# Choosing the keys of three long tiles in the retention stage instead of in sparse attention, with a reordered entry into the feed-forward part

## The chip, the cores and the metric

One core of a Trainium2 chip runs the whole program. The metric is the device time of one execution in microseconds (us), from which medians are taken over several runs. The engines are called TensorE (PE in the rows), VectorE (DVE), ScalarE (ACT), GpSimd (POOL) and SyncE (SP, which only issues transfers).

## The reference, cut to what matters

Two layers of a streaming encoder over one prompt of 1024 frames and 8 running streams of 16 frames. Both layers do the same:

- an input projection, split among three mixers that read the same rows;
- mixer A: a gated MLP that mixes positions within chunks of 128;
- mixer B: sparse attention. An indexer scores every admissible key for each query, the best 256 are kept (68 for the streams), and six heads attend over those keys;
- mixer C: retention, six heads in the chunkwise recurrent form, with a state that decays from chunk to chunk, a norm for each head and a gate;
- an output projection, `x = LN(ALPHA * x + mix @ w_out)`, then `x = LN(ALPHA * x + ffn(x))`, where the feed-forward part gates an up projection with a short causal convolution.

```python
score = jnp.where(adm[None], score, -jnp.inf)
_, idx = lax.top_k(score, k_sel)
logits = jnp.where(valid[:, :, None, None, :], logits, -jnp.inf)
p = jax.nn.softmax(logits, axis=-1).astype(v.dtype)

def step(r, kv_n):
    return chunk_decay[None, :, None, None] * r + kv_n, r
```

## The kernel before, in words

**Tiles.** The 1024 prompt rows are eight tiles of 128 rows and the 128 stream rows are a ninth. In the program's order tile number `DEC` = 4 is the streams', `G1` = 0 to 4 and `G2` = 5 to 8; in the score and attention code i = 0 to 7 counts prompt tiles and i = 8 the streams. Every product of float32 numbers is made of three matmuls with parts that split each operand exactly (`mm3`, L176 to L178); the high part is a cast on ScalarE, the low part a subtraction on VectorE or GpSimd (`put`, L1224; `load_slab`, L105).

**Order.** The text of the program sets a priority: an instruction that stands earlier in it is preferred. A planner runs over the whole program and writes one fixed order for each engine from these priorities and from its own estimate of when operands are ready. `high_priority(offset=-1500)` puts what it holds behind everything else that is ready; `issue_after(ins)` keeps what it holds behind one instruction of the same engine. On the chip every engine then works in the order written for it and waits where an operand is missing.

**One layer** has these stages: indexer and mixer A, retention, sparse attention in two parts, output projection and first norm, feed-forward entry, feed-forward loop over 22 column blocks, down projection and second norm.

**Selection.** Three searches, one for each group in `SETS` = ((2, 3, 4), (6, 7), (5, 8)), find each row's threshold bit by bit. They run during retention at the low priority (`searches`, `advance`, `chain`). After its search a tile is selected (`select`, L616): an equality test, a running count, two comparisons and one last step that turns 0 and 1 into a bias of the logits (L622 to L628), all on VectorE. A tile that isn't in `LATE` is selected in `chain`, still in retention, in place over its scores. A tile in `LATE` is selected in sparse attention, after the projection of a tile in `HEAVYJ` (`b_proj`, L891), into its own bias tile. Tiles 4 to 7 that are not in `LATE` are copied into their bias tiles at the end of the first part (L1129 to L1132), since the scores' memory is given up there.

**Retention** (`c_qk`, `c_turn`, `c_vg`, `c_out`, `c_norm`) goes over three head pairs p and nine tiles. `c_out` keeps the state: VectorE adds the new product to the decayed state `gR`, and GpSimd makes `gR` from the state (L777). `c_norm(2, 5)`, the last norm, is wholly on VectorE. The tiles of sparse attention's first part take the memory that retention gives up.

**Sparse attention, first part.** The projections of nine tiles are 19 steps (`steps`); `work()` makes the next one. `FIRST` of them come at once, the rest as filler in units of attention: after a unit in `EXTRA`, in the stream units in `DFILL`, and after chunk c of tile i where (i, c) stands in `FILLS`. A unit is `look` (logits, bias and minimum on VectorE L958, exponential on ScalarE L960, reciprocal, scale L962) and `gather` (turn the weights, copy them in two parts L991 and L992, multiply with the values L969 and L970). `look_dec` and `gather_dec` (L1059) are the like for streams. **Second part:** tiles 4 to 7, whose filler is the output projection of `G1`. The scale is on GpSimd for i of 4 and up.

**Output projection and norm.** `w_out` adds into the rows (L1163). `norm1(j)` of a tile in `G2` takes mean and variance (`row_stats`, L223 and L224), adds EPS on VectorE (L211), takes the power on GpSimd (L212), makes the bias on VectorE (L231) and applies both on ScalarE (L232).

**Feed-forward entry.** The product with the two weight halves is made of seven products (a Strassen-like form), whose operands are sums of row halves and sums of weight blocks. `half1(j)` makes the row operands of tiles in `G1`, `pair(j)` those of the others: eight turns on TensorE (L1236), four recovered blocks (L1276), eight affine steps on ScalarE (L1290), then sums on VectorE (L1292 to L1298), each split by `put`. The first sum `t1` lies in `tail` for all pairs. `pair` returns `rest`, which splits the last two sums. `wnext()` makes the next weight operand: for S2 three sums and for S4 one on GpSimd (L1358 to L1362), which also use `tail`, then a cast (L1364) and a subtraction (L1365); on its way it issues the next loads on SyncE (`raw_load`, L1341). Four `wnext` come after `w_out(8, 2)` and four after `w_out(8, 3)`; then come the products `early` (A11, A12 of block 0), a copy of the first to free its bank (L1449), `pair(8)`, two more products, and the rests.

```python
        early("A11", 0, "B11")
        nc.scalar.copy(s1, first["A11", 0][:, :, :288])
        early("A12", 0, "B21")
        rests.append(pair(8, where(), where()))
        early("A11", 1, "B11")
        early("A12", 1, "B21")
```

Of the kernel before, what the change touches and what calls it, by code (L numbers as in the profile page):

```python
# [37 lines left out]
LATE = (4, 5, 6, 7)  # L38
WOP = 7
FIRST = 5  # L40
EXTRA = (0, 2, 4)
DFILL = (0, 1, 2, 3)
FILLS = ((0, 0), (1, 0), (2, 0), (2, 1), (3, 3), (4, 1), (5, 1), (6, 1), (7, 1), (6, 5), (7, 5))
LOOKF = (4, 5, 6, 7)
HEAVYJ = (2, 3, 4, 7)
# [22 lines left out]
def hybrid_encoder(ctx: ExitStack, tc: tile.TileContext, d: dict):  # L68
# [145 lines left out]
    def row_stats(r, sp, st=None):  # L214


        halves = (0, 1) if st is None else (1,)
        if st is None:
            st = sp.tile([P, 2, 6], F32, tag="bnst", name="bnst", bufs=2)
        mv = sp.tile([P, 2], F32, tag="bnmv", name="bnmv", bufs=2)  # L220
        sc = sp.tile([P, 2], F32, tag="bnsc", name="bnsc", bufs=2)
        for c in halves:
            nc.vector.bn_stats(st[:, c, :], r[:, c * 512:(c + 1) * 512])  # L223
        nc.vector.bn_aggr(mv, st)  # L224
        rstd_of(sc[:, 0:1], mv[:, 1:2])
        return mv, sc

    def norm_rows(r, sp, st=None):

        mv, sc = row_stats(r, sp, st)  # L230
        nc.vector.scalar_tensor_tensor(sc[:, 1:2], mv[:, 0:1], -1.0, sc[:, 0:1], op0=ALU.mult, op1=ALU.mult)  # L231
        nc.scalar.activation(r, r, AF.Identity, bias=sc[:, 1:2], scale=sc[:, 0:1])  # L232
# [44 lines left out]
    for L in range(d["layers"]):  # L277
# [471 lines left out]
        def c_out(p, j, st):  # L749
# [3 lines left out]
            if j != DEC:  # L753
# [21 lines left out]
                if j < NT - 1:  # L775
                    st["gR"] = gR = cw.tile([P, P], F32, name="gR")
                    nc.gpsimd.tensor_scalar(gR, Rn, gch[:, 0, p:p + 1], None, op0=ALU.mult)  # L777
# [164 lines left out]
        def look(i, par, wp):  # L942
# [6 lines left out]
            for hh in range(3):  # L949
# [12 lines left out]
                (nc.vector if i < 4 else nc.gpsimd).tensor_scalar(pr[:, :w], pr[:, :w], st[:, 1:2], 1.0, op0=ALU.mult, op1=ALU.mult)  # L962
# [183 lines left out]
        lnT = ct[0][:, 1024:1040].rearrange("p (a k) -> p a k", a=2)  # L1146
        nc.sync.dma_start(lnT, d["ln1T"][L])
        bnj = {j: ct[0][:, 1040 + 12 * n:1052 + 12 * n].rearrange("p (c s) -> p c s", c=2) for n, j in enumerate(G2)}
# [75 lines left out]
        def put(at, n, src, eng):  # L1224

            nc.scalar.copy(at(n, 0), src)
            eng.tensor_tensor(at(n, 1), src, at(n, 0).bitcast(F32), ALU.subtract)
# [51 lines left out]

        def pair(j, where, rec):  # L1280
# [4 lines left out]
            t1, t2, t3 = (t.rearrange("p (k t) -> p k t", k=4) for t in (tail[:, 0:512], *temps))  # L1285
            temps[:] = x1s[j][:, 0:512], x1s[j][:, 512:1024]
            b11, b21 = whole(at, ("B11", "B21"), rec)
            for k0, t, v in ((0, t3, va), (4, t2, vb)):
                for k in range(4):
                    nc.scalar.activation(t[:, k, :], v[:, k, :], AF.Identity, bias=lnT[:, 1, k0 + k:k0 + k + 1],  # L1290
                                         scale=lnT[:, 0, k0 + k:k0 + k + 1])
# [4 lines left out]
            V.tensor_tensor(t2, t2, t1, ALU.subtract)  # L1296
            put(at, "T2", t2, V)
            V.tensor_tensor(t2, b21, t2, ALU.subtract)  # L1298

            def rest():  # L1300
                put(at, "T3", t3, V)
                put(at, "T4", t2, V)

            return rest
# [39 lines left out]
        def wnext():  # L1344
# [11 lines left out]
            src = {"A11": a11, "A12": a12, "S1": tail[:, 0:512], "S2": a11, "S3": a21, "S4": a12, "A22": a22}[n]  # L1356
            if n == "S2":
                G.tensor_tensor(tail[:, 0:512], a21, a22, ALU.add)  # L1358
                G.tensor_tensor(a21, a11, a21, ALU.subtract)
                G.tensor_tensor(a11, tail[:, 0:512], a11, ALU.subtract)  # L1360
            if n == "S4":
                G.tensor_tensor(a12, a12, a11, ALU.subtract)  # L1362
# [21 lines left out]
        for u, (s, j) in enumerate(todo_w):  # L1384
# [19 lines left out]
            if s == 3 and j > 5:  # L1404
                rests.append(pair(j - 1, where(), where()))
            if j == 8 and s >= 2:
# [44 lines left out]
        rests.append(pair(8, where(), where()))  # L1451
# [3 lines left out]
        for r in rests:  # L1455
            r()
# [363 lines left out]
```

## Time and profile before

| | |
|---|---|
| median of 3 runs | 2881.7 us (2879.95 to 2882.68) |
| the profiled execution | 2882.72 us, of which the span from first to last instruction is 2880.9 |
| mean granted clock of TensorE | 0.988 |
| TensorE busy | 2793.0 us, 97% of the span, 19444 matmuls |
| VectorE busy | 2061.6 us, 72% |
| ScalarE busy | 1387.3 us, 48% |
| GpSimd busy | 886.3 us, 31% |

The matmuls are pipelined, so a busy TensorE need not be at its peak. Idle time of another engine costs nothing by itself. In the rows a line is L and its number, a tile has the program's name without its buffer number, and `<-` stands between what is written and what is read; a wait is put down to what ended it. The two layers start at 0 and about 1430 us, and the second repeats the first's waits at much the same places.

### The profile page before, as it was taken

How to read it: one execution, taken by the hardware profiler on the slowest of the kernel's cores; microseconds unless marked ns; L12 is line 12 of the kernel's file. 1: busy time of each engine (PE TensorE's matmuls, PEld its weight loads, DVE VectorE, ACT ScalarE, POOL GpSimd, SP SyncE). 2: the span in 40 equal slices, each digit the busy share in tenths (PEclk: the TensorE clock that was granted, in tenths of full speed). 3: DMA queues.
4: the chain of work that ended last, by engine and by line, in shares of the span. 5: the costliest groups of instructions: out<-in, count | busy, mean ns of one | idle time of the engine just before them, and what ended most of it. 6: DMA issues, size and time to landing. Idle time of an engine off the chain costs nothing. (4 is left out here: it accounts for less than half of the span.)

```text
span 2880.9 us, 51251 instructions
## 1 busy us (share of the span) xinstructions
PE 2793.0 (97%) x19444; PEld 2613.9 (91%) x19444; DVE 2061.6 (72%) x4580; ACT 1387.3 (48%) x2937; POOL 886.3 (31%) x891
## 2 busy tenths in 40 slices
PE   8999999998999999999999999989989999999998
PEld 8898898998999999888898988989889999997886
DVE  6899878768666666556678997787686666665656
ACT  5687656645333333421256885565553333334211
POOL 2334543443322232000433445334432223220003
PEclk9999999999999999999999999999999999999999
DMA  4121123132212222443212111231322121224421
GB/s 138 53 66 50 43 62 102 58 125 92 72 70 76 76 79 96 158 131 127 79 47 81 39 50 47 56 111 47 121 94 77 69 85 70 72 100 155 153 84 66
DMA packets 105013, 243.15 MB, mean 84 GB/s; under 512 B 21671, under 2 KB 42047, under 8 KB 104767
## 3 DMA queue, kind: packets, MB, share of 16 engines
q1 hardware_dynamic: 88014, 198.59, 21.3%
q10 hardware_dynamic: 16752, 41.29, 3.7%
q8 instruction: 153, 2.51, 0.3%
q14 instruction: 94, 0.76, 0.1%
HBM read 185.20 MB, written 54.64 MB: 83 GB/s over the span
## 5 line engine op out<-in xcount | busy, mean ns | idle before, releaser
L176 PE MATMUL pg<-ar,ring 128*128 128x288 f32 x1408 | 417.1, 296 | 10.1 <-ACT s L1449 4.2
L178 PE MATMUL pg<-ar,ring 128*128 128x288 f32 x1408 | 417.2, 296 | 0.0
L177 PE MATMUL pg<-ar,ring 128*128 128x288 f32 x1408 | 416.5, 296 | 0.0
L1364 ACT CAST ring<-raw 128x512 fp32r<-128x512 f32 x264 | 163.3, 622 | 422.8 <-PE pg L177 401.6
L128 POOL TENSOR_TENSOR ring<-raw,ring 128x512 fp32r<-128x512 f32 (+1 forms) x140 | 191.7, 1396 | 317.9 <-ACT ring L127 270.1
L571 ACT ACTIVATE spare<-sc,cand 128x896 bf16<-128x896 f32 (+5 forms) x262 | 244.7, 934 | 67.3 <-DVE cand L598 21.2
L176 PEld LDWEIGHTS pg<-ar,ring 128*128 128x128 f32 x1408 | 266.1, 189 | 11.7 <-ACT s L1449 4.6
L1365 DVE TENSOR_TENSOR ring<-raw,ring 128x512 fp32r<-128x512 f32 x264 | 203.7, 776 | 90.9 <-ACT ring L1364 90.9
L177 PEld LDWEIGHTS pg<-ar,ring 128*128 128x128 f32 x1408 | 266.2, 189 | 0.0
L178 PEld LDWEIGHTS pg<-ar,ring 128*128 128x128 f32 x1408 | 266.0, 189 | 0.0
L1540 DVE TENSOR_TENSOR s<-s,pg 128x576 f32<-128x576 f32 x220 | 164.4, 749 | 50.8 <-PE pg L178 48.3
L1650 DVE TENSOR_TENSOR acc<-acc,pdn 128x512 f32<-128x512 f32 x180 | 121.3, 683 | 89.3 <-PE pdn L178 88.7
L1484 DVE TENSOR_TENSOR hx<-s,pg 128x512 f32<-128x512 f32 x88 | 60.5, 688 | 150.5 <-PE pg L178 150.5
L176 PE MATMUL pwo<-ring,ar 128*128 128x256 f32 x576 | 166.9, 290 | 0.0
L177 PE MATMUL pwo<-ring,ar 128*128 128x256 f32 x576 | 163.8, 284 | 0.0
L178 PE MATMUL pwo<-ring,ar 128*128 128x256 f32 x576 | 163.8, 284 | 0.0
L565 DVE TENSOR_SCALAR_CACHE_REDUCE spare<-sc,cand 128x384 bf16<-128x384 f32 (+4 forms) x208 | 158.5, 762 | 1.9
L176 PE MATMUL pdn<-ring,ar 128*128 128x512 f32 x360 | 140.1, 389 | 0.0
L177 PE MATMUL pdn<-ring,ar 128*128 128x512 f32 x360 | 140.1, 389 | 0.0
L178 PE MATMUL pdn<-ring,ar 128*128 128x512 f32 x360 | 140.1, 389 | 0.0
L1489 ACT ACTIVATE ct<-hx,cwt 128x512 f32<-128x512 f32 x88 | 71.8, 816 | 127.7 <-DVE hx L1484 127.7
L176 PE MATMUL pvg<-ring,ar 128*128 128x256 f32 x432 | 127.8, 296 | 1.4 <-DVE sg L740 1.4
(427 smaller groups left out, 9434.7 us busy)
## 6 DMA issues: line engine op xcount, KB each, us to landing
raw<-w_gu SPq DMA_DIRECT2D x90, 512.0 KB, 3.8
ad<-ct ACTq DMA_DIRECT2D x44, 576.0 KB, 2.8
raw<-w_d SPq DMA_DIRECT2D x44, 512.0 KB, 4.3
raw<-w_s SPq DMA_DIRECT2D x40, 512.0 KB, 3.9
raw<-w_o SPq DMA_DIRECT2D x32, 512.0 KB, 4.0
araw<-ad SPq DMA_DIRECT2D x48, 288.0 KB, 3.0
s<-ad SPq DMA_DIRECT2D x40, 288.0 KB, 3.6
x1d<-x ACTq DMA_DIRECT2D x18, 512.0 KB, 2.6
```

The lines of the kernel that those rows point to most:

```text
L128: eng.tensor_tensor(l[:, t], raw[:, r], h[:, t].bitcast(F32), ALU.subtract)
L176: nc.tensor.matmul(out, lh, rh, start=first, stop=False)
L177: nc.tensor.matmul(out, lh, rl, start=False, stop=False)
L178: nc.tensor.matmul(out, ll, rh, start=False, stop=last)
L565: nc.vector.tensor_scalar(junkv[:, :w], sc[i], cand[q][:, c:c + 1].bitcast(F32), float(kof(i) - w), op0=ALU.is_lt, op1=ALU.add, accum_out= ...
L571: nc.scalar.activation(junka[:, :w], sc[i], AF.Sign, bias=cand[q][:, c:c + 1].bitcast(F32), scale=-1.0, accum_out=dst)
L1364: nc.scalar.copy(h, src)
L1365: V.tensor_tensor(l, src, h.bitcast(F32), ALU.subtract)
L1484: V.tensor_tensor(hp.rearrange("p (c n) -> p c n", c=2), prompt(sv), prompt(b), ALU.add)
L1489: nc.scalar.activation(cf[:, 512 * h:512 * h + 512], hp, AF.Identity, **kw)
L1540: V.tensor_tensor(out, a, b[:, :, :288], ALU.add)
L1650: V.tensor_tensor(acc[j][:, cs], acc[j][:, cs], po, ALU.add)
```

## The change

Four kinds of edits. First, of the four long tiles only tile 7 stays in `LATE`, and it is selected after the first projection (`HEAVYJ` = (0,)); tiles 4, 5 and 6 are selected in retention and copied later. Second, the fillers of sparse attention's first part are placed elsewhere: one place less in `EXTRA` and `DFILL`, and (3, 1) in place of (2, 1) in `FILLS`. Third, for the last head pair the decayed state is made on ScalarE, and for the last look of tile 7 the scale is made on VectorE. Fourth, at the feed-forward entry: the norm of a `G2` tile has all three small steps on GpSimd; `t1` has two buffers in `ct[0]` by turns, and the small vectors that lay there go to `tail`; the sums of weight blocks are on VectorE for block 0; four of the eight early `wnext` come after `pair(8)`, their casts behind its affine steps and their three sums behind its sum before T2; the rests of all pairs come as casts behind the affine steps of pair 8 and subtractions behind its T2.

```diff
-LATE = (4, 5, 6, 7)
+LATE = (7,)
-EXTRA = (0, 2, 4)
-DFILL = (0, 1, 2, 3)
-FILLS = ((0, 0), (1, 0), (2, 0), (2, 1), (3, 3), (4, 1), (5, 1), (6, 1), (7, 1), (6, 5), (7, 5))
+EXTRA = (0, 2)
+DFILL = (0, 1, 2)
+FILLS = ((0, 0), (1, 0), (2, 0), (3, 1), (3, 3), (4, 1), (5, 1), (6, 1), (7, 1), (6, 5), (7, 5))
-HEAVYJ = (2, 3, 4, 7)
+HEAVYJ = (0,)
...
-        rstd_of(sc[:, 0:1], mv[:, 1:2])
+        if len(halves) == 1:
+            nc.gpsimd.tensor_scalar(sc[:, 0:1], mv[:, 1:2], EPS, None, op0=ALU.add)
+            nc.gpsimd.tensor_tensor(sc[:, 0:1], sc[:, 0:1], mhalf[:, 0:1], ALU.pow)
+        else:
+            rstd_of(sc[:, 0:1], mv[:, 1:2])
...
-        nc.vector.scalar_tensor_tensor(sc[:, 1:2], mv[:, 0:1], -1.0, sc[:, 0:1], op0=ALU.mult, op1=ALU.mult)
+        if st is None:
+            nc.vector.scalar_tensor_tensor(sc[:, 1:2], mv[:, 0:1], -1.0, sc[:, 0:1], op0=ALU.mult, op1=ALU.mult)
+        else:
+            nc.gpsimd.tensor_scalar(sc[:, 1:2], mv[:, 0:1], sc[:, 0:1], -1.0, op0=ALU.mult, op1=ALU.mult)
...
-                    nc.gpsimd.tensor_scalar(gR, Rn, gch[:, 0, p:p + 1], None, op0=ALU.mult)
+                    if p == 2:
+                        nc.scalar.activation(gR, Rn, AF.Copy, scale=gch[:, 0, p:p + 1])
+                    else:
+                        nc.gpsimd.tensor_scalar(gR, Rn, gch[:, 0, p:p + 1], None, op0=ALU.mult)
...
-                (nc.vector if i < 4 else nc.gpsimd).tensor_scalar(pr[:, :w], pr[:, :w], st[:, 1:2], 1.0, op0=ALU.mult, op1=ALU.mult)
+                (nc.vector if i < 4 or (i, par) == (7, 1) else nc.gpsimd).tensor_scalar(
+                    pr[:, :w], pr[:, :w], st[:, 1:2], 1.0, op0=ALU.mult, op1=ALU.mult)
...
-        lnT = ct[0][:, 1024:1040].rearrange("p (a k) -> p a k", a=2)
+        lnT = tail[:, 512:528].rearrange("p (a k) -> p a k", a=2)
...
+        t1s = ct[0][:, 0:512], ct[0][:, 512:1024]
...
-            t1, t2, t3 = (t.rearrange("p (k t) -> p k t", k=4) for t in (tail[:, 0:512], *temps))
+            t1, t2, t3 = (t.rearrange("p (k t) -> p k t", k=4) for t in (t1s[j % 2], *temps))
...
-            V.tensor_tensor(t2, t2, t1, ALU.subtract)
-            put(at, "T2", t2, V)
+            hold["sum"] = V.tensor_tensor(t2, t2, t1, ALU.subtract)
+            hold["split"] = put(at, "T2", t2, V)
             V.tensor_tensor(t2, b21, t2, ALU.subtract)
 
-            def rest():
-                put(at, "T3", t3, V)
-                put(at, "T4", t2, V)
-
-            return rest
+            rests.extend(((at, "T3", t3), (at, "T4", t2)))
...
+            e = G if f else V
             if n == "S2":
-                G.tensor_tensor(tail[:, 0:512], a21, a22, ALU.add)
-                G.tensor_tensor(a21, a11, a21, ALU.subtract)
-                G.tensor_tensor(a11, tail[:, 0:512], a11, ALU.subtract)
+                with ExitStack() if f else tc.issue_after(hold["sum"].ins):
+                    e.tensor_tensor(tail[:, 0:512], a21, a22, ALU.add)
+                    e.tensor_tensor(a21, a11, a21, ALU.subtract)
+                    e.tensor_tensor(a11, tail[:, 0:512], a11, ALU.subtract)
             if n == "S4":
-                G.tensor_tensor(a12, a12, a11, ALU.subtract)
+                e.tensor_tensor(a12, a12, a11, ALU.subtract)
...
-            if j == 8 and s >= 2:
+            if (s, j) == (2, 8):
                 for _ in range(4):
                     wnext()
...
-        rests.append(pair(8, where(), where()))
+        pair(8, where(), where())
+        for _ in range(4):
+            with tc.issue_after(hold["affine"].ins):
+                wnext()
         early("A11", 1, "B11")
         early("A12", 1, "B21")
         rest_dec()
-        for r in rests:
-            r()
+        for at, n, t in rests:
+            with tc.issue_after(hold["affine"].ins):
+                nc.scalar.copy(at(n, 0), t)
+            with tc.issue_after(hold["split"].ins):
+                V.tensor_tensor(at(n, 1), t, at(n, 0).bitcast(F32), ALU.subtract)
```

## Rows read from the trace of the kernel before

**Rows 1.** Busy time by stretch: length, PE, PEld, DVE, ACT, POOL, PEclk, DMA

```profile
347.00:376.00 29.00, 29.00 (x232) 26.01 (x231) 14.87 (x38) 6.87 (x21) 17.63 (x16) 1.00 0.19 59
376.00:480.00 104.00, 93.38 (x747) 87.78 (x746) 85.56 (x235) 71.27 (x226) 34.69 (x38) 0.97 0.25 75
400.00:425.00 25.00, 21.61 (x179) 21.32 (x178) 24.78 (x64) 14.53 (x51) 7.01 (x7) 0.89 0.13 38
570.00:600.00 30.00, 26.75 (x198) 25.73 (x197) 26.54 (x60) 17.93 (x32) 18.37 (x14) 0.94 0.18 74
636.00:676.00 40.00, 31.07 (x223) 29.01 (x222) 33.11 (x59) 28.91 (x59) 13.02 (x14) 0.95 0.23 81
700.00:1180.00 480.00, 480.00 (x3559) 476.74 (x3558) 319.33 (x525) 188.16 (x299) 131.40 (x141) 1.00 0.25 85
...
1806.00:1912.00 106.00, 94.29 (x735) 88.74 (x734) 85.96 (x233) 70.70 (x221) 34.84 (x38) 0.94 0.24 74
...
2070.00:2116.00 46.00, 37.23 (x262) 35.42 (x260) 37.25 (x63) 33.94 (x69) 13.84 (x15) 0.93 0.24 86
```

**Rows 2.** TensorE's waits, 376 to 480 us: us in total, times, longest

```profile
PE tpd L1059 <- DVE ast L958: 3.4, 1, 3.4
...
PE pb L176 <- DVE ast L958: 1.4, 1, 1.4
```

**Rows 3.** The eight half-clock stretches, TensorE alone: one, and the sum

```profile
671.93:678.75 6.82, 5.41 (x22) 0.50 0.48 157
...
sum 40.95, PE 33.84; mean PE 4.23
```

**Rows 4.** VectorE on the bias tiles, 376 to 470 us; two steps by form

```profile
376.00:470.00 94.00, 24.72 (x20) 0.96 0.23 67
...
L627 DVE SCALAR_TENSOR_TENSOR bias<-sc,cand,bias 128x896 bf16<-128x896 f32 x1 | 3.3, 3301 | 0.0
...
L627 DVE SCALAR_TENSOR_TENSOR bias<-sc,cand,bias 128x1024 bf16<-128x1024 f32 x1 | 1.3, 1266 | 0.0
```

**Rows 5.** Timeline of ScalarE and TensorE where sparse attention begins

```profile
375.80 0.27 ACT L901 COPY kv<-pb 128x128 f32<-128x128 f32 x1 [4.55 <-DVE yb L819]
...
378.88 0.22 PE L173 MATMUL kt<-identr,kss 128*128 128x128 f32 x1
```

**Rows 6.** TensorE's waits, 570 to 600 us

```profile
PE po L969 <- ACT pth L991: 1.6, 1, 1.6
PE tp L988 <- POOL pr L962: 1.4, 1, 1.4
```

**Rows 7.** TensorE's waits at the first layer's feed-forward entry, 636 to 676 us

```profile
PE pg L176 <- ACT s L1449: 4.2, 1, 4.2
PE trx L1236 <- ACT x L232: 3.1, 2, 1.7
PE trx L1276 <- DVE x L1298: 1.4, 1, 1.4
```

**Rows 8.** TensorE's waits at the second layer's, 2070 to 2116 us

```profile
PE pg L176 <- DVE x L1298: 4.1, 1, 4.1
...
PE pg L176 <- ACT x L1290: 1.6, 1, 1.6
```

**Rows 9.** Timeline of ScalarE, VectorE and GpSimd at the first layer's entry

```profile
640.45 2.56 ACT L1290 ACTIVATE temp<-trx,ct 128x128 f32<-128x128 f32 x7 [0.75 <-PE trx L1236]
...
664.73 0.68 DVE L1227 TENSOR_TENSOR ar<-x,ar 128x512 fp32r<-128x512 f32 x1
...
665.50 1.60 DVE L1227 TENSOR_TENSOR art<-x,art 128x512 fp32r<-128x512 f32 x1
...
664.95 1.60 POOL L1358 TENSOR_TENSOR tail<-raw 128x512 f32<-128x512 f32 x1 [3.08 <-ACT ar L1226]
...
671.61 1.14 ACT L1364 CAST ring<-raw 128x512 fp32r<-128x512 f32 x2 [1.05 <-POOL raw L1362]
672.65 0.63 ACT L1449 COPY s<-pg 128x576 f32<-128x576 f32 x1
```

More of the change, by code (lines that the diff above doesn't have):

```diff
@@ L1145, in hybrid_encoder @@
         s1 = xp1.tile([P, 2, 288], F32, name="s1")
-        lnT = ct[0][:, 1024:1040].rearrange("p (a k) -> p a k", a=2)
+        lnT = tail[:, 512:528].rearrange("p (a k) -> p a k", a=2)
         nc.sync.dma_start(lnT, d["ln1T"][L])
-        bnj = {j: ct[0][:, 1040 + 12 * n:1052 + 12 * n].rearrange("p (c s) -> p c s", c=2) for n, j in enumerate(G2)}
+        bnj = {j: tail[:, 528 + 12 * n:540 + 12 * n].rearrange("p (c s) -> p c s", c=2) for n, j in enumerate(G2)}
         xg1s = ExitStack()
@@ L1226, in put @@
             nc.scalar.copy(at(n, 0), src)
-            eng.tensor_tensor(at(n, 1), src, at(n, 0).bitcast(F32), ALU.subtract)
+            return eng.tensor_tensor(at(n, 1), src, at(n, 0).bitcast(F32), ALU.subtract)
         def turned_x(src, where):
@@ L1289, in pair @@
                 for k in range(4):
-                    nc.scalar.activation(t[:, k, :], v[:, k, :], AF.Identity, bias=lnT[:, 1, k0 + k:k0 + k + 1],
+                    hold["affine"] = nc.scalar.activation(t[:, k, :], v[:, k, :], AF.Identity, bias=lnT[:, 1, k0 + k:k0 + k + 1],
                                          scale=lnT[:, 0, k0 + k:k0 + k + 1])
@@ L1404, in hybrid_encoder @@
             if s == 3 and j > 5:
-                rests.append(pair(j - 1, where(), where()))
-            if j == 8 and s >= 2:
+                pair(j - 1, where(), where())
+            if (s, j) == (2, 8):
                 for _ in range(4):
```

## The prediction

> **What bounds the kernel now.** I read the busy times by stretch first, then TensorE's waits in the stretches that show gaps, then the granted clock, and last the instructions at a few of those waits. In the feed-forward loop TensorE is never idle: 3559 matmuls fill 480 us, 0.135 us each [rows 1]. So nothing there can be won, and the change does not touch its steady part. The gaps lie in a few places of each layer: 10.6 us of 104 in sparse attention's first part, 3.25 of 30 near its end, 8.9 of 40 where the feed-forward part begins; the second layer has 11.7 of 106 and 8.8 of 46 in the like places [rows 1], and its own copy of the 3.25. Together that is 46.5 us. In the middle of the first of them VectorE works 24.78 of 25 us while TensorE stands for 3.4 [rows 1], and the two longest waits there end with VectorE [rows 2]. So VectorE, which is far from full over the whole run, is the bound in just these places.
>
> A second price hangs on them. The granted clock is 0.50 (1.2 of 2.4 GHz) in eight stretches of 3.4 or 6.8 us in or just behind these gaps, and TensorE is busy for 33.84 us of them [rows 3]. There 22 matmuls take 5.41 us, 0.246 each, against 0.135: 45% of busy time is lost, 15.2 us in all, 1.9 a stretch. The ceiling of the change is thus about 62 us.
>
> **Selection moved (LATE, HEAVYJ).** Choosing the keys of tiles 4 to 7 in sparse attention costs VectorE 24.7 us a layer, 20 steps of 1.2 on average [rows 4]. By width (640, 768 and 896 of 3328 columns) 69% of it, 17 us, goes into retention. Three copies into the bias tiles come in its place, on VectorE under projections; if that cover is gone they cost at most the average step each, 3.7 us. Tile 7's selection, the other 7.7 us, moves forward to the first projection, where four projections' matmuls are queued on TensorE; I neither credit nor charge it. Of the waits I credit those that end with the softmax minimum behind selection, 3.4 and 1.4 us, in both layers: 9.6. What is left of the idle time, 5.8 and 6.9 us, comes from the chain through three engines in tile 3's units, where no projection was left as filler.
>
> **Projections spread out (EXTRA, DFILL, FILLS).** Nothing is added: the 19 steps stay. By counting them, steps that came earlier now stand in the gathers of tile 3. Earlier units lose filler just as they lose VectorE's selection work. I credit a third of the rest, 1.9 and 2.3: 4.2 (ends 0 and 12.7). Of the clock, the two stretches behind the 3.4 us waits go wholly, two more in the second layer by a third: 1.3 + 3.8 = 5.1. This part: 18.9 us.
>
> **Price in retention.** Its last 29 us have 14.87 us of VectorE work, 14.1 free [rows 1], for 17 us of selection, at a lower priority than the rest. The overflow is 3 us. Sparse attention begins only when VectorE's last norm frees memory: ScalarE stood 4.55 us for it, and TensorE first needed the result 3.1 us after that wait ended [rows 5]. An instruction once begun is not interrupted, so the norm's steps queue behind selection steps of 1 to 2 us. Taken: 2.5 a layer, 5 in all (ends: none, and the third rival's price). The decayed state of the last head pair goes from GpSimd to ScalarE, which is busy 6.87 of 29 us there [rows 1]; no matmul waits for it in the rows: nothing, up to 1 us if ScalarE's queue is full.
>
> **Last softmax scale on VectorE.** TensorE waits 1.4 us for GpSimd's product there and then 1.6 for ScalarE's copy [rows 6]. VectorE is at 26.54 of 30 us, so the three products may only shift the wait. I take half of the 1.4, 0.7 a layer: 1.4 (ends 0 and, with the copy and its clock stretch, 4.9 a layer).
>
> **Entry of the feed-forward part.** The norm's chain now goes VectorE, GpSimd, VectorE, ScalarE; afterwards it stays on GpSimd before ScalarE. Two waits for it make 3.1 us a layer [rows 7]; one hop fewer of three, and no place in VectorE's queue: half of it, 1.55 a layer, 3.1 (ends 0 and 6.2). On GpSimd's queue the three steps stand among the stream pair's sums; it is busy 13.02 of 40 us there [rows 1], so I charge nothing. The load of the norm's vectors keeps its place on SyncE's queue and only changes its target.
>
> The other waits there are 4.2 + 1.4 in the first layer, 4.1 + 1.6 in the second [rows 7, 8]: 11.3. The trace shows what made them. A subtraction takes VectorE 0.68 us alone and 1.60 beside GpSimd's sum of 1.60; ScalarE's casts wait for GpSimd's sums, and the copy that frees TensorE's bank comes behind them, ending at 673.28 [rows 9]. The change takes all three causes away: sums of tile 0 on VectorE, four weight steps and all second halves behind pair 8's affine steps, two buffers for the first sums. SyncE's loads for the next tile move back with the weight steps; their first user is five products, 16 us, later, so that is covered.
>
> But something else is late next. From pair 8's transposes TensorE has two products, 48 matmuls, 6.5 us, until it needs the weight sum S2. The way to it: eight affine steps (2.56 us for seven, so 2.9 [rows 9]), four VectorE steps and three sums of 0.68, a cast of about 0.6 and a last 0.68: 8.9 us. A new wait of 2.4 stands in each layer. Net 11.3 - 4.8 = 6.5. Of the two clock stretches, 3.8, I credit half, 1.9. This part: 3.1 + 6.5 + 1.9 = 11.5 (ends: 21.3 if no wait follows, none if S2's wait takes everything back).
>
> Behind the waiting casts on ScalarE and sums on VectorE stand the second halves of the pairs, which the third to fifth product read: 7 us and more later.
>
> **The sum.** 18.9 + 1.4 + 11.5 - 5.0 = 26.8 us off the profiled execution's 2882.7 (span 2880.9): 2855.9. That execution lies 1.0 over the median of the runs shown, 2881.7, so 2855.
>
> **Rivals.** *Every gap closes* (0.20): the waits leave no follower and the clock stays up. Then of the 62 us some three quarters go, 46, and retention takes nothing back: 2836. For it: the waits share one cause. Against: the last third of sparse attention's gaps is a chain of engines, not load.
>
> *Selection was not the bound* (0.22): with filler taken from early units TensorE waits there for the same softmax, and of sparse attention only a third is won, 6; with 1.4 and 11.5, less 5, 14 us: 2868. For it: the units that lose filler are those with the 3.4 us wait.
>
> *Retention becomes VectorE's bound* (0.06), slower than before. The selection steps run at contended length: one on 896 columns takes 3.30 us, its like on 1024 only 1.27 [rows 4]. GpSimd works 17.63 of 29 us there, against 34.69 of 104 in sparse attention [rows 1]. At 2.2 times, 17 us become 37; less 14.1 free and 3.1 of slack, 20 us stall a layer, and a clock stretch makes 22. Both layers: 44, against 32 won: slower by 12, 2894. It decides from a stall of 16 a layer on. Against: TensorE is busy for all of retention's last 29 us [rows 1], although tiles 2, 3 and 8 are chosen in retention already. The Trainium skill, "SBUF — State Buffer", section "Who interferes with whom", makes this a rule: a VectorE instruction with two SBUF inputs, or one in a two-port mode, and a GpSimd instruction that reads SBUF shut each other out for a whole instruction. By that rule, moving selection to where GpSimd works more is wrong; the subtraction of 1.60 us beside GpSimd's 1.60 [rows 9] agrees with it. Taken whole it would give the rival's 2894 and not 2855; no run here shows what it costs TensorE.
>
> *The order hardly changes* (0.07): the planner puts the moved steps where they stood, and gains and price cancel: 2881.
>
> **How the numbers follow.** The forecast has 0.45. A measurement here tells about 0.2%, 5.8 us, from no change. Faster are the forecast, every gap closes and the selection rival: 0.87; the same 0.07; slower 0.06. Likeliest: 2855. The range holds the first three with a share of the unknown costs, from 2833 to 2877.
>
> **What would show it.** Right: no wait over 1 us for the softmax minimum in sparse attention's first units; no selection step behind its first projections except tile 7's; TensorE idle there under 5 us a layer; clock stretches down from eight to about four; at the entry a wait of some 2 us for S2 instead of 4.2 and 4.1; retention's last 29 us with VectorE near full. Wrong: sparse attention starting more than 5 us later after retention, new waits of the retention products for VectorE, or new half-clock stretches behind the S2 wait.

## The result and the profile after

The changed kernel takes 2901.43 us (median of 4 runs, 2899.35 to 2903.46), the kernel before 2882.19 on the same chip: a ratio of 1.0064, 95% interval 1.0052 to 1.0076. It is slower by 19.2 us, where 26.8 less were forecast. The profiled execution has a span of 2901.6 us against 2880.9. TensorE is busy for 2794.9 us of it, against 2793.0: of the 20.7 us more, 18.8 are idle time of TensorE. So new waits, not new work, made the loss.

The busy time by stretch of the changed kernel (columns as in [rows 1]; the first three stretches are the same, the last two longer, since the entry is):

```profile
347.00:376.00 29.00, 23.35 (x174) 20.18 (x173) 28.34 (x54) 7.12 (x23) 14.40 (x10) 0.93 0.03 10
376.00:480.00 104.00, 99.37 (x817) 96.55 (x817) 75.14 (x225) 71.84 (x227) 33.11 (x42) 0.97 0.28 80
570.00:600.00 30.00, 25.57 (x186) 24.64 (x185) 27.11 (x57) 16.34 (x29) 14.69 (x10) 0.89 0.17 71
636.00:700.00 64.00, 46.95 (x321) 45.04 (x320) 41.18 (x69) 37.34 (x75) 15.70 (x23) 0.89 0.18 62
2070.00:2140.00 70.00, 49.32 (x334) 47.41 (x333) 40.27 (x68) 36.90 (x74) 16.99 (x25) 0.88 0.17 57
```

Sparse attention's first part came out as meant: 4.6 us idle of 104 instead of 10.6, VectorE down from 85.56 to 75.14. The stretch before it lost what it had: TensorE, never idle in retention's last 29 us before, stands for 5.65 there, and VectorE is full. At the entry TensorE is idle for 17 of 64 us and 21 of 70.

TensorE's waits of the changed kernel, 340 to 480 us, the largest group (us in total, times, longest):

```profile
PE py L766 <- DVE Rb L777: 4.9, 2, 4.6
```

and 570 to 710 us:

```profile
PE pg L176 <- ACT ring L1375: 9.4, 1, 9.4
PE tp L999 <- DVE bnsc L211: 4.2, 1, 4.2
PE trx L1247 <- ACT x L239: 3.3, 1, 3.3
PE pg L176 <- DVE s L1557: 2.3, 1, 2.3
```

No wait for the softmax minimum is left ([rows 2] had 3.4 and 1.4). In their place stand one for the retention state (py), one for the last weights of tile 7 (tp, where [rows 6] had 1.4 and 1.6), one for the norm (trx, 3.3 for the 3.1 of [rows 7]) and the longest of all, 9.4 us before the first product with S2. The second layer repeats the four of them with 4.65, 4.23, 3.26 and 9.39 us, and has a fifth, before the first product of the entry and behind the last sum of a pair (L1311, L1298 before), where [rows 8] had 4.1:

```profile
PE pg L176 <- DVE x L1311: 5.3, 1, 5.3
```

The half-clock stretches, TensorE alone (granted clock 0.50 in each): thirteen in these places where [rows 3] had eight. Two of them, behind the waits for the state and for S2:

```profile
371.89:378.72 6.83, 5.29 (x25) 0.50 0.07 14
682.50:692.74 10.24, 5.88 (x24) 0.50 0.38 116
```

Stage by stage, from the start of each stage's first matmul in the two traces (layer one, layer two; us more than before; in the second layer the border between the third row and the fourth moves by up to 0.5 us with the matmul taken for it):

| stage | measured | forecast, both layers |
|---|---|---|
| retention, up to the first turn of keys | +9.2, +6.8 | +5.0 |
| sparse attention's first part from there | -9.9, -11.8 | -18.9 |
| second part (last scale on VectorE) | +1.1, +2.0 | -1.4 |
| norm, up to the recovered blocks of pair 5 | +2.6, +2.2 | -3.1 |
| the rest: entry, loop, down projection | +8.0, +13.9 | -8.4 |
| second layer's indexer stage | -3.3 | 0 |

### The profile page after: what moved, and what is told of

It reads as the page before. It is cut to its first block, busy times and chain, and to the rows that moved or that the text cites. A ratio compares the mean times of both kernels' runs of the same rounds, so it can differ in the third digit from the quotient of the medians.

```text
span 2901.6 us, 51222 instructions
## 1 busy us (share of the span) xinstructions
PE 2794.9 (96%) x19444; PEld 2622.1 (90%) x19444; DVE 2062.8 (71%) x4584; ACT 1391.4 (48%) x2951; POOL 860.3 (30%) x879
## 5 line engine op out<-in xcount | busy, mean ns | idle before, releaser
L128 POOL TENSOR_TENSOR ring<-raw,ring 128x512 fp32r<-128x512 f32 (+1 forms) x140 | 185.5, 1351 | 355.1 <-ACT ring L127 305.3
```

The source lines that it names most:

```text
L128: eng.tensor_tensor(l[:, t], raw[:, r], h[:, t].bitcast(F32), ALU.subtract)
```

## The experiments

Sixteen kernels ran, each beside runs of the kernel before on the same chip, so the ratio with its interval is what compares them (it differs from the quotient of the two medians by up to 0.07%).

| run | us | before | ratio, 95% interval |
|---|---|---|---|
| a_rests_free | 2894.8 | 2882.7 | 1.0048 [1.0033, 1.0063] |
| b_attention | 2880.1 | 2882.7 | 0.9995 [0.9986, 1.0005] |
| b_entry | 2895.2 | 2882.7 | 1.0048 [1.0033, 1.0063] |
| b_norm_scale | 2889.2 | 2882.7 | 1.0024 [1.0013, 1.0036] |
| fill_only | 2896.8 | 2882.1 | 1.0049 [1.0036, 1.0061] |
| late_67 | 2879.5 | 2882.1 | 0.9987 [0.9978, 0.9996] |
| gr_pool | 2877.9 | 2882.1 | 0.9981 [0.9972, 0.9990] |
| bufs_sums | 2888.1 | 2882.1 | 1.0018 [1.0009, 1.0027] |
| two_bufs | 2893.1 | 2882.6 | 1.0043 [1.0029, 1.0057] |
| entry_rests_free | 2889.4 | 2882.6 | 1.0025 [1.0015, 1.0034] |
| late_47 | 2877.2 | 2882.6 | 0.9984 [0.9975, 0.9992] |
| late_47_w | 2879.3 | 2882.6 | 0.9991 [0.9982, 1.0000] |
| one_buf_ct | 2890.1 | 2885.5 | 1.0020 [1.0011, 1.0030] |
| bufs_tail8 | 2884.6 | 2885.5 | 1.0001 [0.9992, 1.0010] |
| sums_only | 2882.2 | 2885.5 | 0.9990 [0.9980, 1.0000] |
| late_47_sums | 2878.9 | 2885.5 | 0.9982 [0.9973, 0.9990] |

### The change taken apart

**b_attention, b_entry, b_norm_scale**: the kernel before with one group of the edits each: selection, fillers and decayed state; the entry; the norm's small steps and the last scale.

> The kernel before with only the selection of tiles 4 to 6 in retention, the fillers' places and the decayed state on ScalarE. If the stages of the changed kernel add up: retention's end up to the turn of the keys +9.2 and +6.7 us, the rest of sparse attention's first part -9.9 and -11.8, so 2876 us, between 2872 and 2881, against 2882.2, with one wait of 4.7 us of the retention products for VectorE's state in each layer. Rival (the stages don't add up, the loss in retention needs the other edits too): no such wait, and 2860 to 2866.

> The kernel before with only the edits of the feed-forward entry: two buffers for the first sums, sums of S2 on VectorE, four weight steps and the second halves behind pair 8. Theory: it holds the main loss, a wait of some 9 us before the first S2 product in each layer, 2900 us, between 2895 and 2905. Rival (the wait needs the norm on GpSimd as well, which makes everything in the entry later): a wait of under 6 us and 2885 to 2892.

> The kernel before with only the norm's small steps on GpSimd and the last scale of tile 7 on VectorE. From the stages of the changed kernel: the scale +1 to +2 us a layer with one wait of about 4 us at the last transposes of the weights, the norm +2 to +3 a layer with one wait of about 3 us instead of two of 1.4 and 1.7: 2889 us, between 2885 and 2893. Rival (the norm's place on GpSimd helps when the rest of the entry is as before): 2881 or less.

Measured: -2.6, +12.5 and +6.5 us, together +16.4 of the 19.2. The first shows the waits expected (4.65 us for the state in each layer) and lies in the range expected; from no change it can't be told. The entry holds the main loss, with the wait of 9.38 us alone and no help from the norm. The third fell as expected, and its trace divides it: +1.2 and +1.8 us for the scale's stage, +2.6 and +2.2 for the norm's. Its rival (the norm helps when the rest is as before) is out.

### The wait for S2

What stands in the queues ahead of it, from the timeline of the changed kernel (start us, length, engine, line, operation, tiles, count, idle before):

```profile
672.98 1.18 ACT L1471 CAST ar<-temp 128x512 fp32r<-128x512 f32 x2
674.01 2.22 ACT L1471 CAST ar<-x 128x512 fp32r<-128x512 f32 x4
676.10 0.66 ACT L1237 CAST arb<-ct 128x512 fp32r<-128x512 f32 x1
679.44 0.69 DVE L1370 TENSOR_TENSOR raw<-raw 128x512 f32<-128x512 f32 x1
680.65 1.29 DVE L1473 TENSOR_TENSOR ar<-temp,ar 128x512 fp32r<-128x512 f32 x2
681.86 3.09 DVE L1473 TENSOR_TENSOR ar<-x,ar 128x512 fp32r<-128x512 f32 x5
685.47 0.68 DVE L1371 TENSOR_TENSOR raw<-tail,raw 128x512 f32<-128x512 f32 x1
686.86 0.61 PE L176 MATMUL pg<-art,ring 128*128 128x288 f32 x1 [9.38 <-ACT ring L1375]
```

The second halves of the pairs (L1471, L1473), which other products need only later, go first on both engines: six casts, 3.4 us, ahead of pair 8's own, and seven subtractions, 4.4 us, between the second sum of S2 (679.44) and the third (685.47). `issue_after` holds them behind pair 8's affine steps and its T2, but nothing holds them behind S2, and the planner placed them as soon as they were let go.

**a_rests_free**:

```diff
         for at, n, t in rests:
-            with tc.issue_after(hold["affine"].ins):
-                nc.scalar.copy(at(n, 0), t)
-            with tc.issue_after(hold["split"].ins):
-                V.tensor_tensor(at(n, 1), t, at(n, 0).bitcast(F32), ALU.subtract)
+            put(at, n, t, V)
```

> The changed kernel, but the second halves of all pairs (T3, T4) are made as before: nothing holds them behind pair 8. Theory (the place of these halves makes the wait): TensorE's wait before the first S2 product falls from 9.4 us to 2 to 3 in each layer, the wait of 2.3 to 2.8 us for the next weight subtraction goes, and with them about 2 us of half clock a layer: 2885 us, between 2880 and 2890, against 2901.4. Rival (the sums of S2 on VectorE make it, VectorE is full there whatever the order): the wait stays at 7 us or more and the time at 2897 or more.

TensorE's waits for the same two things in this run, 636 to 725 us:

```profile
PE pg L176 <- DVE s L1554: 3.1, 2, 2.1
PE pg L176 <- ACT ring L1375: 2.7, 1, 2.7
```

The wait falls from 9.4 to 2.7 us (2.25 in the second layer): the theory of the place holds, VectorE was not full whatever the order. But the loss against the kernel before fell by 7.1 us only, from 19.2 to 12.1, and not by 16, so the time lies above the range expected. A wait for VectorE comes at a later product instead of the 2.3 and 2.8 us of the changed kernel, 2.1 us in the first layer and 5.1 in the second, and the rest of the entry's loss lay elsewhere.

### The parts of the entry

**two_bufs** is the kernel before with the first of these edits (and the small vectors moved as in the change); **bufs_sums** has both; **entry_rests_free** is the whole entry with the second halves free as in a_rests_free.

```diff
-            t1, t2, t3 = (t.rearrange("p (k t) -> p k t", k=4) for t in (tail[:, 0:512], *temps))
+            t1, t2, t3 = (t.rearrange("p (k t) -> p k t", k=4) for t in (t1s[j % 2], *temps))
...
+            e = G if f else V
-                G.tensor_tensor(tail[:, 0:512], a21, a22, ALU.add)
+                e.tensor_tensor(tail[:, 0:512], a21, a22, ALU.add)
...
```

> The kernel before with two of the entry's edits: two buffers for the first sums (and the small vectors moved for it), and the sums of block 0 on VectorE. The eight weight steps and the second halves of the pairs stay where they were. If GpSimd's sums and the one buffer made the waits of 4.2 and 4.1 us, these fall under 2 us, no wait before the first S2 product comes up, and the time is 2870 to 2876. Rival (the waits only move on to ScalarE's casts and affine steps): the waits in the entry add up to what they were, within 2 us a layer, and the time is 2879 to 2886. If it is above 2890, these two edits and not the moved weight steps carry what is left of the entry's loss.

> The kernel before with one edit of the entry: two buffers for the first sums, with the small vectors that move for it; the weight sums stay on GpSimd. Theory (the one buffer had kept GpSimd's sums of the next block off pair 8: they could not write the shared tile until pair 8 was done with it): these sums now run beside pair 8's subtractions, which take 1.8 us instead of 0.7, TensorE waits 2 us or more before the first product with T2, and the time is 2884 to 2889 against 2882. Rival (the six to eight us of the two edits come from VectorE's three sums of block 0 alone): no such wait, 2882 or less.

> The kernel before with all edits of the entry, but the second halves of the pairs left free as before. It closes the sum: two buffers and sums on VectorE cost 6 us, all edits together 12.5 us. If the held second halves carry the rest, the time is 2886 to 2890, with a wait of 2 to 3 us before the first S2 product instead of 9.4. Rival (the four weight steps behind pair 8 carry it): 2892 to 2897, although that wait is gone.

Each against the kernel before beside it: two buffers +10.5 us; with the sums on VectorE +6.0; with four weight steps behind pair 8 as well +6.8; with the second halves held +12.5. So the sums win some 4.5 back, the weight steps cost nothing that can be seen (the intervals of those two overlap), and the hold costs 5.7. I had booked the two buffers as a gain, and they are the dearest single part. I had it wrong once more in the expectations: bufs_sums lies above its range and its rival's, two_bufs above the 2889 of its theory; only entry_rests_free came out as expected. The timeline of GpSimd, VectorE and ScalarE in two_bufs at pair 8:

```profile
678.35 0.69 DVE L1227 TENSOR_TENSOR ara<-x,ara 128x512 fp32r<-128x512 f32 x1
678.54 1.64 POOL L1360 TENSOR_TENSOR tail<-raw 128x512 f32<-128x512 f32 x1 [11.74 <-DVE arb L1227]
678.95 1.79 DVE L1227 TENSOR_TENSOR ar<-x,ar 128x512 fp32r<-128x512 f32 x1
680.66 1.77 DVE L1298 TENSOR_TENSOR x<-x,ct 128x512 f32<-128x512 f32 x1
682.35 1.76 DVE L1367 TENSOR_TENSOR ring<-tail,ring 128x512 fp32r<-128x512 f32 x1
683.60 0.62 ACT L1366 CAST ring<-raw 128x512 fp32r<-128x512 f32 x1 [2.76 <-POOL raw L1362]
684.12 0.61 ACT L1226 CAST art<-x 128x512 fp32r<-128x512 f32 x1
```

and in the kernel before at the same place:

```profile
680.68 0.69 DVE L1296 TENSOR_TENSOR x<-x,tail 128x512 f32<-128x512 f32 x1
681.40 0.62 ACT L1226 CAST art<-x 128x512 fp32r<-128x512 f32 x1 [1.36 <-DVE x L1296]
681.50 1.29 POOL L1358 TENSOR_TENSOR tail<-raw 128x512 f32<-128x512 f32 x1 [9.93 <-DVE x L1296]
```

Before, GpSimd's first sum for block 1 writes `tail`, where pair 8's first sum lies, and so waits until VectorE has read it for T2 (L1296). The shared tile was a lock that kept GpSimd off pair 8's chain. With a buffer of its own the pair no longer holds GpSimd back: its sums start 3 us earlier and VectorE's steps take 1.77 instead of 0.69 us beside them. T2's sum (L1298) is over at 682.43 instead of 681.37, but its cast comes at 684.12 instead of 681.40: ScalarE has a weight cast ahead of it (683.60), which waits 2.76 us for GpSimd's third sum. So of the 2.7 us more, 1.1 are VectorE's slower steps and the rest is the place in ScalarE's queue; before, the casts of these sums stood behind T2's. TensorE waits for T2. Its waits at this entry, 636 to 725 us, in two_bufs, without the two for the norm, which are those of [rows 7]:

```profile
PE trx L1276 <- DVE x L1300: 4.9, 1, 4.9
...
PE pg L176 <- ACT art L1226: 1.9, 1, 1.9
PE pg L177 <- DVE art L1227: 1.3, 1, 1.3
```

By the Trainium skill, "SBUF — State Buffer", section "Who interferes with whom", a VectorE instruction with two SBUF inputs and a GpSimd instruction that reads SBUF shut each other out; the 1.79 us beside the sum of 1.64 agree with that.

**one_buf_ct** and **bufs_tail8** test the lock: one buffer, but away from `tail`; and two buffers, of which pair 8's is `tail` again.

```diff
-        t1s = ct[0][:, 0:512], ct[0][:, 512:1024]
+        t1s = ct[0][:, 0:512], ct[0][:, 0:512]
```

```diff
-        t1s = ct[0][:, 0:512], ct[0][:, 512:1024]
+        t1s = tail[:, 0:512], ct[0][:, 512:1024]
```

> The kernel before with the first sums of all pairs in one buffer of their own, away from the tile in which the weight sums lie; the small vectors move as in the change. If the shared tile had been what held GpSimd's weight sums back, this costs what two buffers cost: 2889 to 2896 against 2882.5, with VectorE's subtractions at 1.6 to 1.8 us beside GpSimd's sums both in pair 7's and in pair 8's steps. Rival (the second buffer is the cause): 2884 or less.

> The kernel before with two buffers for the first sums, of which that of pairs 6 and 8 is the shared tile again. GpSimd's sums of block 1 then wait for pair 8 as before, those of block 0 no longer wait for pair 7. If each of the two places carries its part, the wait before the first product with T2 (1.9 + 1.3 us with two buffers) goes, the wait of 4.9 us at pair 8's recovered blocks stays, and the time is 2885 to 2889. Rival (only the sums of block 0, beside pair 7, matter): 2890 or more. Rival (only those of block 1): 2883 or less.

In one_buf_ct these three waits of the first layer are 4.9, 1.5 and 1.3 us. In bufs_tail8 they are

```profile
PE trx L1276 <- DVE x L1300: 5.6, 1, 5.6
PE pg L177 <- DVE art L1227: 0.8, 1, 0.8
```

and the longest of the second layer's entry is there

```profile
PE pg L176 <- DVE x L1300: 8.3, 1, 8.3
```

where two_bufs and one_buf_ct have 8.5 and [rows 8] had 4.1. From pair 5's recovered blocks to the first matmul of the down projection, us more than before:

| run | layer one | layer two |
|---|---|---|
| two_bufs | +5.6 | +4.6 |
| one_buf_ct | +4.5 | +4.8 |
| bufs_tail8 | -0.8 | +4.9 |
| five runs that leave the entry as it was | -0.6 to +3.1 | +0.3 to +3.1 |

One buffer has the waits of two, to 0.4 us in the first layer and the same longest in the second: they come from `tail` being free, not from there being two buffers. The time rose by 4.6 us, less than the 10.5 of two_bufs; the intervals of the two meet only at their ends, so whether the second buffer adds something stays open. With pair 8 back in `tail`, GpSimd's sum stands at 681.50 as before, the waits for T2 fall from 3.2 to 0.8 us and the first layer's loss is gone: there, block 1's sums beside pair 8 carry it, and block 0's early sums beside pair 7 cost nothing on balance, since the 5.6 us replace the 1.4 and 4.2 of [rows 7].

In the second layer it is not so. Pair 8's place changes nothing there: the three runs wait alike and lose alike, and what they share is the place of pair 7. That block 0's sums beside pair 7 make this loss fits, but no run shows it, since the same wait is 9 us or more in runs that leave the entry alone (below, *What stays open*). The whole time of bufs_tail8 is that of the kernel before (1.0001), better than I expected; in its trace the first layer's start and the second layer's indexer stage, which the edit doesn't touch, are some 3 us shorter and hide part of the second layer's loss.

**sums_only** (the second half of the diff of bufs_sums alone) and **late_47_w** (on late_47, below) try to shorten the wait of 4.2 us in [rows 7] in other ways.

```diff
-            if j == 8 and s >= 2:
+            if (s, j) == (2, 8):
...
-        nc.scalar.copy(s1, first["A11", 0][:, :, :288])
+        cp = nc.scalar.copy(s1, first["A11", 0][:, :, :288])
+        for _ in range(4):
+            with tc.issue_after(cp.ins):
+                wnext()
```

> The kernel before with only the weight sums of block 0 on VectorE; the first sums stay in the shared tile. With two buffers the sums on VectorE won 5 us (2888.1 against 2893.1). If they win the same here, 2876 to 2879, with the wait of 4.2 us for the copy behind the casts under 2.5 us. Rival (VectorE has no room there, its queue is full beside pairs 7 and 8): 2882 or more, with a wait of 4 us or more behind VectorE's steps.

> The run with tiles 4 and 7 left in sparse attention, and at the entry four weight steps (S2, S1, S4, S3 of block 0) put behind the copy that frees TensorE's bank, instead of ahead of it. If ScalarE's casts behind GpSimd's sums made the wait of 4.2 us for that copy, it falls under 1.5 us in each layer and the time is 6 to 10 us under that run's. Rival (the wait moves to the weight sums, which now come later): a new wait of 2 us or more before the first S2 product, and the time within 4 us of that run's.

Neither does much. With the tile kept, the sums on VectorE give at most 0.2%: the wait for the copy falls to 3.4 and that for the recovered blocks grows from 1.4 to 1.9. Weight steps behind the copy bring the rival: the wait before a later product with S2 grows from none over 0.15 us to 1.9 in layer one and from 1.0 to 2.6 in layer two, and nothing is won over late_47.

### Retention and the fillers

What holds the state back, from the timeline of the changed kernel:

```profile
369.84 1.40 DVE L633 SCALAR_TENSOR_TENSOR both<-spare,need,both 128x392 bf16<-128x392 f16 x1
370.78 4.38 POOL L128 TENSOR_TENSOR ring<-raw,ring 128x512 fp32r<-128x512 f32 x3
371.28 1.51 DVE L634 SCALAR_TENSOR_TENSOR both<-sc,cand,both 128x392 bf16<-128x392 f32 x1
372.71 0.57 DVE L777 SCALAR_TENSOR_TENSOR Rb<-pkv,gch,gR 64x64 f32<-64x64 f32 x2
373.43 0.77 PE L766 MATMUL py<-Rb,qkT 128*128 128x128 f32 x2 [4.65 <-DVE Rb L777]
```

VectorE chooses tiles 6, 5, 4 and 8 one after the other, with retention's own short steps between and no pause. The last, 392 columns wide, stands ahead of the state's update (L777), and its steps run at 1.40 and 1.51 us beside GpSimd's work, mostly weight subtractions (L128). In the kernel before the same two steps took 1.44 and 1.29 us, but tile 8 was done at 347.3 us, and no matmul waited.

**gr_pool** is b_attention with the decayed state left on GpSimd. **late_67** is b_attention, **late_47** gr_pool with one tile more kept in sparse attention (6 or 4; late_47's line is shown). **fill_only** has only the fillers' places.

```diff
-LATE = (7,)
+LATE = (4, 7)
-HEAVYJ = (0,)
+HEAVYJ = (0, 2)
```

> The kernel before with the selection and filler edits, the decayed state of the last head pair left on GpSimd. Theory (nothing waits for it): the wait of 4.65 us in retention within 0.5 us of the same, 2877 to 2883, as with the decayed state on ScalarE (2880.1). Rival (ScalarE's queue makes the state late): the wait falls by 1 us or more and the time to 2872 or less; or (GpSimd is full) it grows and the time is 2886 or more.

> The kernel before with the selection and filler edits, but only tiles 4 and 5 are selected in retention; 6 and 7 stay in sparse attention, behind the first and third projection. If the price in retention is the amount of selection (tile 6 took VectorE 10 us there), the wait of 4.65 us of the retention products for VectorE's state falls under 1 us, the turn of the keys comes within 2 us of before, and if sparse attention's first part keeps two thirds of its gain the time is 2866 to 2872. Rival (the order does it: the last tile's selection stands ahead of the state's update however much is selected): a wait of 3 us or more stays and the time is 2876 or more.

> The kernel before with the selection and filler edits and the decayed state left on GpSimd, but only tiles 5 and 6 are selected in retention; 4 and 7 stay in sparse attention. If VectorE's queue at retention's end is some 4 us too long, tile 4's steps (4.4 us there) are enough: the wait of 4.75 us for the state falls under 1 us, the turn of the keys comes within 2 us of before, sparse attention's first part keeps 7 us or more a layer: 2866 to 2873. Rival (tile 8's selection, the last one, stands ahead of the state whatever is taken out): the wait stays over 3 us, 2876 or more.

> The kernel before with only the fillers of sparse attention's first part placed as in the change; tiles 4 to 7 are still selected there. If the places of the fillers won the 9.9 and 11.8 us of that part, it keeps 6 us or more a layer, retention costs nothing, and the time is 2866 to 2872 against 2882.7. Rival (the selection steps were the bound, the fillers alone do nothing or harm, since early units lose filler while VectorE still selects): that part within 2 us of before or longer, 2880 to 2890.

gr_pool has the same wait, 4.76 us (4.65 with ScalarE), and the intervals of the two overlap: no price of who makes the decayed state shows. In late_47 the wait is all but gone (last line), and the steps of the same tile run at their free length, since they now come ahead of GpSimd's work:

```profile
359.88 0.62 DVE L626 SCALAR_TENSOR_TENSOR both<-spare,need,both 128x392 bf16<-128x392 f16 x1
361.14 0.62 DVE L627 SCALAR_TENSOR_TENSOR both<-sc,cand,both 128x392 bf16<-128x392 f32 x1
...
PE py L759 <- DVE Rb L770: 0.8, 2, 0.5
```

The amount decides, and 4 us of it are enough: counted from retention's start, both late runs have the turn of keys within 2 us of before. Yet both stay above what was expected (2879.5 and 2877.2 where 2873 was the most), each only 0.6 or 0.7 us under the run that it was made from: the selection kept in sparse attention takes back gain there, where late_47 wins 4.4 and 7.1 us a layer, and late_67 3.8 and 6.3, instead of 9.9 and 11.8.

fill_only went against both expectations in size. The fillers alone lose 14.7 us, of which 6.2 and 3.5 in sparse attention's first part; TensorE's two longest waits there:

```profile
PE tp L988 <- DVE pr L962: 4.1, 1, 4.1
PE tpd L1059 <- POOL pr L1047: 4.0, 2, 3.4
```

The units that gave up filler wait for the softmax, whose steps VectorE still makes between selections. The fillers' new places win only together with the selection's move: the gain of 9.9 and 11.8 us is no sum of two terms. What the selection's move wins with the fillers where they were, more or less than that, no run shows.

**late_47_sums**, late_47 with the weight sums of sums_only, was the try for a version that beats both.

> The version with tiles 4 and 7 left in sparse attention, and the weight sums of block 0 on VectorE. If the parts add up, it is as far under 2877.2 as the run with the sums alone is under 2882.5: 2871 to 2875 if that wins, and then it is the best of all. Rival (the order of the entry comes out otherwise and the parts don't add up): 2877 or more.

By its time it falls under the rival, but the kernel before was 3 us slower on that chip. By the ratios the two parts together would give 0.9974; measured is 0.9982, and its interval just holds the other, so whether they add stays open. gr_pool, late_47_sums and late_47, 0.19%, 0.18% and 0.16% under the kernel before, are the best seen; the intervals do not part the three.

## Why the prediction was wrong

**Selection and fillers, -18.9: right in sum.** 21.7 us were measured, and the waits that I named are gone. The division into a term for selection and one for filler was not right, so that the sum came out so near is in part luck; fill_only shows that the second does not exist by itself.

**Price in retention, +5.0: mis-sized, 16 measured.** The step that failed compared 17 us of work with 14.1 us of free time over the whole stretch and left an overflow of 3. The amount was right: the steps of tiles 4 to 6 took 17.2 us there. But they came ahead of tile 8's selection in VectorE's order. That one, done at 347.3 us before, now ran from 367 to 374 and stood ahead of the state that TensorE needed next; late_47 shows that some 4 us less of work ahead of it are enough. The term looked at the norm's memory as the only thing waiting there; that TensorE's own products wait for VectorE's state stood in the rival and the signs alone. The rival *Retention becomes VectorE's bound* had this mechanism at 22 us a layer; 9.2 and 6.8 were measured. The state's move to ScalarE, put at nothing, shows no cost.

**Last scale, -1.4: wrong sign, +1.2 and +1.8 alone.** I saw that the wait might only shift and still booked half of it. Two of the three products of 1024 columns do gain by the move, 0.75 and 0.74 us on VectorE where GpSimd took 1.12. The last, the one that TensorE waits for, does not: it takes VectorE 1.76 us with GpSimd at work beside it, and GpSimd had made it in 1.11 (last line, the kernel before). TensorE waits once for 4.23 instead of 1.4 and 1.6 (the waits above put it down to L211, a small step right behind the product):

```profile
575.43 0.74 DVE L972 TENSOR_SCALAR pr<-pr,ast 128x1024 f32<-128x1024 f32 x1
...
587.09 1.76 DVE L972 TENSOR_SCALAR pr<-pr,ast 128x1024 f32<-128x1024 f32 x1
585.95 2.35 POOL L244 TENSOR_TENSOR x<-x,ct 128x1024 f32<-128x1024 f32 x1 [2.22 <-DVE bnsc L236]
...
586.38 1.11 POOL L962 TENSOR_SCALAR pr<-pr,ast 128x1024 f32<-128x1024 f32 x1
```

**Norm on GpSimd, -3.1: wrong sign, +2.6 and +2.2 alone.** "I charge nothing" for GpSimd's queue was the failing step. The three small steps stand each behind a sum of the streams' pair:

```profile
637.05 0.21 DVE L224 BATCH_NORM_AGGREGATE bnmv<-tail 128x2 f32<-128x12 f32 x1
637.42 0.25 POOL L226 TENSOR_SCALAR bnsc<-bnmv 128x1 f32<-128x1 f32 x1
637.64 0.74 POOL L1275 TENSOR_TENSOR x4d<-ar,x4d 128x256 f32<-128x256 f32 x1
638.34 0.57 POOL L227 TENSOR_TENSOR bnsc<-bnsc,mhalf 128x1 f32<-128x1 f32 x1
...
639.55 0.72 POOL L1276 TENSOR_TENSOR x4d<-x4d,ar 128x256 f32<-128x256 f32 x1
640.37 0.27 POOL L238 TENSOR_SCALAR bnsc<-bnmv,bnsc 128x1 f32<-128x1 f32 x1
```

Mean and variance are ready at 637.26, the bias only at 640.64: 1.1 us of steps took 3.4. A busy share of 13 of 40 us said nothing about a chain that passes the queue three times. The row of the stages holds only the first of the two waits that the term counted; by waits alone, 3.1 us before are 3.3 in the changed kernel and 3.9 and 3.3 in b_norm_scale, so nothing was won either way.

**The other waits of the entry, -6.5 and -1.9 of clock: wrong sign, +12.5 alone.** Two steps failed. "The change takes all three causes away" had two buffers among the cures, and two_bufs alone costs 10.5 us: the shared tile was a lock, and in the first layer one_buf_ct and bufs_tail8 show that it kept GpSimd's sums, and the casts that wait for them, behind pair 8's own steps. And the chain to S2, 8.9 us for a new wait of 2.4, is right as a chain: with the second halves free the wait measures 2.7. But the prediction took it that these come behind the chain; 3.4 us of them on ScalarE and 4.4 on VectorE stood inside it, and the wait was 9.4. The hold cost 5.7 us of the entry's 12.5. What the second halves had cost before, when nothing held them, was never asked. And in the second layer the wait of 4.1 us that the term booked as gone is one of 5.3, and the two half-clock stretches of the two entries, of which it took half as saved, became seven.

**The chances.** No rival was right. The slower one had the right sign and a wait that did come, in retention, but the attention edits together broke even (b_attention). No rival priced the entry as a loss, and the entry's own worst end was nothing won; that is why even the slower rival's 2894 lies below the result. Of the signs named at the end, the wrong ones all came: sparse attention later by 7.4 us, the retention products waiting for VectorE, half-clock stretches behind S2's wait.

**What stays open.** The entry's order came out otherwise in runs that did not touch it: in fill_only the first product there waits for 9.7 us, in before for 0.2, with other work ahead of it, and b_attention waits 9.2 us in its second layer. Differences of a few us a layer between such runs are not put down to one edit here; nor are the 3.3 us of the second layer's indexer stage, nor what the changed kernel loses at the second layer's entry (+13.9 with the loop) beyond the 7.2 us that b_entry loses there.

## What to carry to other kernels

A buffer that two engines share is also an order between them: before you give each its own, look at what the wait kept apart, in the queues of third engines too. Work that is held back in order to clear a path needs a second bound, behind the thing it must not delay; held only until the path begins, it is placed in the path. And free time of an engine over a stretch prices nothing: ask which instruction will stand directly ahead of the one that TensorE waits for, and how often a chain passes the queue that it is moved to.

## What the hardware showed that was not expected

The same step of VectorE on 392 columns takes 0.62 us (late_47) or 1.40 to 1.51 us (the changed kernel, beside GpSimd's work): the place alone makes a factor of 2.3 to 2.4. A product of one input by a column, on 1024 columns, took 1.76 us with GpSimd at work beside it and 0.74 without (L972). And GpSimd pays as well: its power step on a single column takes 0.57 us at 638.34 and 1.40 at the end of sparse attention, beside a VectorE sum of 1024 columns:

```profile
589.06 1.40 POOL L212 TENSOR_TENSOR bnsc<-bnsc,mhalf 128x1 f32<-128x1 f32 x1 [0.76 <-DVE bnsc L211]
```
